# The operand pairs of a seven-product feed-forward: differences on GpSimd, casts behind a copy of the next tile

## The chip, the cores and the metric

One core of one Trainium2 chip. The metric is the device time of one execution in microseconds; lower is better. The kernel before took 2896.02 us, the median of three runs (2888.88 to 2900.18).

## The reference, cut to what matters

One inference step of a two-layer decoder trunk on 576 columns (512 of a prompt, 64 of eight samples), model width 1024, feed-forward width 2816. Each layer has two feed-forward parts; the change touches the first of layer 0 and the second of layer 1.

```python
def swiglu(x, wi, wo):
    gate, up = jnp.split(x @ wi, 2, axis=-1)
    return (jax.nn.silu(gate) * up) @ wo
...
h = h + 0.5 * swiglu(rms_norm(h, w['norm_w'][i, 0]), w['ffn1_wi'][i], w['ffn1_wo'][i])
```

## The kernel before

Everything is kept transposed, 128 features by 576 columns a tile, in two halves of 288 columns. A matrix product in float32 is made of three passes: each operand is split into a rounded part H, a cast on ScalarE, and a remainder L = x - H, a subtraction on DVE or GpSimd, and TensorE sums H*H + H*L + L*H. `split` (L161) does this for moving operands.

A feed-forward part (`ffn`, L395 on) makes 22 tiles j of 128 hidden features: gate and up, silu, their product u (128x576). The first five tiles use plain products (`pair`). From tile 5 on `pair7` (L427) makes gate and up of both column halves as one 2x2 block product with seven products in place of eight, each of 4 x 3 = 12 matmuls of 128x288. In the text the seven are counted in the order in which TensorE runs them. Results are built up in three PSUM banks A, C, B: a bank is copied out by ScalarE (`copy`, L440, its instruction L442) or added to a copy by DVE (`add`, L445, its instruction L448) before the next product adds to it. So the third product waits for the copy of the first, the fifth for the copy of the third, and the seventh for DVE's addition that reads the fifth. After the silu (L152), u is the product of up and silu, one half on DVE (L484), the other on GpSimd (L485).

The weights of a tile are formed by `seven` (L331): four raw blocks come in by DMA on SP's queue, DVE makes four sums and differences of them (L358, L369; the first and third read two SBUF blocks, the others also PSUM), ScalarE casts each of the seven forms (L350), and DVE or GpSimd makes the remainders (L353; forms 0, 3 and 6 on GpSimd). Forms of the next tile are made while a tile runs, as buffers come free.

Two of the four feed-forward parts are "deep" (`deep=True`): their second product, h += 0.5 * (u @ wo), also runs as seven products from the seventh hidden tile on (`wo_part7`, L507). It runs once after tile 14, for tiles 6 to 13, and once after tile 21, for tiles 14 to 21, each time for n = 0, 2, 4, 6. For it two tiles of u, a (even j) and b (odd j), are made into seven moving operands by `pair_forms` (L376): four differences of 128x288 (L382 to L385: c = a1 - a0, then b1 - a1, d = b1 - c0, and a1 = b0 - d), then a split of c, a, b and d. It is called when tile b is complete: the differences on DVE, the casts on ScalarE, the remainders on GpSimd (two of them on DVE for the last pair, `quick`). There are eight pairs in a deep part.

The tile framework orders each engine's queue by its own priorities from the program's order and the dependencies; an engine then works its queue strictly in that order. `after` (L157) adds an order between two instructions of one engine.

Of the kernel before, what the change touches and what calls it, by code (L numbers as in the profile page):

```python
# [9 lines left out]
F32R = mybir.dt.float32r  # L10
# [6 lines left out]
D = 1024  # L17
# [6 lines left out]
FT = FF // 128  # L24
# [69 lines left out]
class Body:  # L94
# [65 lines left out]

    def split(self, src, H, L, eng=None):  # L161
        nc = self.nc
        nc.scalar.copy(H, src)
        self.last_l = (eng or nc.vector).tensor_tensor(L, src, H.bitcast(F32), op=ALU.subtract).ins  # L164
        return H, L
# [209 lines left out]

    def pair_forms(self, a, b, quick):  # L376

        nc = self.nc
        h0, h1 = slice(0, HF), slice(HF, T)
        sub = ALU.subtract  # L380
        c, d = self.s("t1", self.n_t1), self.ph.tile([128, HF], F32, name="ev", tag="ev", bufs=N_EV)
        nc.vector.tensor_tensor(c[:, h0], a[:, h1], a[:, h0], op=sub)  # L382
        nc.vector.tensor_tensor(c[:, h1], b[:, h1], a[:, h1], op=sub)
        nc.vector.tensor_tensor(d, b[:, h1], c[:, h0], op=sub)
        nc.vector.tensor_tensor(a[:, h1], b[:, h0], d, op=sub)  # L385
        out = []
        for i, x in enumerate((c, a, b)):
            out.append(self.split(x, self.s("hv", self.n_hv, F32R), self.s("hv", self.n_hv, F32R), nc.vector if quick and i < 2 else nc.gpsimd))
        D = self.ph.tile([128, 2, HF], F32R, name="hv", tag="hv", bufs=self.n_hv)
        self.split(d, D[:, 0], D[:, 1], nc.gpsimd)  # L390
        C, A, B = out
        return [(x[0][:, sl], x[1][:, sl]) for x, sl in ((C, h0), (C, h1))] + [(D[:, 0], D[:, 1])] + \
            [(x[0][:, sl], x[1][:, sl]) for x, sl in ((A, h1), (A, h0), (B, h0), (B, h1))]

    def ffn(self, wi, wo, done, pre=None, mid=None, fast=None, side=None, deep=False):  # L395

        nc = self.nc
        xs, rs = self.xl[0], self.rs
        hv, hist = {}, {}
# [3 lines left out]
        first7 = ends[1] if deep else FT  # L403
        pairs = {}

# [20 lines left out]

        def pair7(j, X):  # L427
            h0, h1 = slice(0, HF), slice(HF, T)
            n = DT // 2 * 128
# [10 lines left out]
            def copy(ps):  # L440
                t = self.ph.tile([128, HF], F32, name="ev", tag="ev", bufs=N_EV)
                nc.scalar.copy(t, ps)  # L442
                return t
# [25 lines left out]
            else:  # L469
# [4 lines left out]
                prod(A, 2, 2, False)  # L474
                u2 = copy(A)
                prod(B, 3, 5, True)
                add(B, p1, t1[:, h0])
# [9 lines left out]
            if j < first7:  # L487
                hv[j] = self.split(u, self.s("hv", self.n_hv, F32R), self.s("hv", self.n_hv, F32R), nc.gpsimd)
            elif (j - first7) % 2 == 0:
                pairs[j] = u  # L490
            else:
                pairs[j - 1] = self.pair_forms(pairs[j - 1], u, j == FT - 1)

# [13 lines left out]
        def wo_part7(js, last):  # L507

            f = done() if last else None
            X = [pairs[j] for j in js[0::2]]  # L510
            h0, h1 = slice(0, HF), slice(HF, T)
            for n in range(0, DT, 2):
                v = [wo[n + a][:, js[0] * 128:(js[-1] + 1) * 128].rearrange("p (i z c) -> p z i c", z=2, c=128) for a in range(2)]
                W = self.seven({f"{a + 1}{b + 1}": v[a][:, b] for a in range(2) for b in range(2)})
                A, C, B = self.bank("e", HF), self.bank("e", HF), self.pg.tile([128, HF], F32, name="ps_d", tag="d")

                def prod(ps, i, x, first, ks=range(len(X))):
# [5 lines left out]
                def to_h(ps, a, sl):  # L523
                    h = self.h[n + a]
                    return nc.vector.scalar_tensor_tensor(h[:, sl], ps, 0.5, h[:, sl], op0=ALU.mult, op1=ALU.add).ins
                if last and not n:
                    steps = ((C, 1, 0), (A, 0, 4), (B, 3, 5))
# [35 lines left out]
        j = 0  # L563
# [1384 lines left out]
```

## Time and profile before

| what | value |
|---|---|
| median of three runs | 2896.02 us (2888.88 to 2900.18) |
| profiled execution, its own time | 2892.69 us |
| its span, first to last instruction | 2890.9 us |
| mean granted TensorE clock | 0.973 |
| busy: TensorE, DVE, GpSimd, ScalarE | 2724.6, 1848.0, 1395.2, 1329.0 us |
| the first deep part, and the second | about 85 to 438 us, and 2463 to 2823 us of the span |

PE is TensorE's matmuls, PEld its weight loads, DVE VectorE, ACT ScalarE, POOL GpSimd, SP SyncE; L numbers are lines of the kernel. In a timeline row stand the start (us from the span's start), the duration, engine, line, operation, output and inputs, shapes, and in brackets the idle time of the engine just before, with what ended it. A row of a table by stretches gives, for each engine, its busy time and the number of instructions, then the granted TensorE clock as a share of 2.4 GHz, the DMA share and GB/s. The list of waits gives, for each pair of who waited and whom for, the total in us, the number of waits and the longest. DVE's rows of successive instructions overlap slightly, as do the others'.

### The profile page before, as it was taken

How to read it: one execution, taken by the hardware profiler on the slowest of the kernel's cores; microseconds unless marked ns; L12 is line 12 of the kernel's file. 1: busy time of each engine (PE TensorE's matmuls, PEld its weight loads, DVE VectorE, ACT ScalarE, POOL GpSimd, SP SyncE). 2: the span in 40 equal slices, each digit the busy share in tenths (PEclk: the TensorE clock that was granted, in tenths of full speed). 3: DMA queues.
4: the chain of work that ended last, by engine and by line, in shares of the span. 5: the costliest groups of instructions: out<-in, count | busy, mean ns of one | idle time of the engine just before them, and what ended most of it. 6: DMA issues, size and time to landing. Idle time of an engine off the chain costs nothing.

```text
span 2890.9 us, 55999 instructions
## 1 busy us (share of the span) xinstructions
PE 2724.6 (94%) x21760; PEld 2539.6 (88%) x21760; DVE 1848.0 (64%) x3683; ACT 1329.0 (46%) x2648; POOL 1395.2 (48%) x1130
## 2 busy tenths in 40 slices
PE   8999997988999999999999999999999999989997
PEld 7999997887767768999999999999888789989987
DVE  6577788557577756553646546352777776477775
ACT  4344445444333225443445445354556654444454
POOL 5555547544243335544544455454444335564543
PEclk9999998998999999999999999999999999999999
DMA  4223234222112112232333223325334533223222
GB/s 134 82 84 88 85 100 138 70 66 54 53 44 77 39 52 85 83 94 87 94 97 97 94 85 96 92 77 143 90 81 113 161 126 98 88 77 94 79 77 92
DMA packets 201758, 257.80 MB, mean 89 GB/s; under 512 B 46937, under 2 KB 101761, under 8 KB 201492
## 3 DMA queue, kind: packets, MB, share of 16 engines
q1 hardware_dynamic: 173888, 224.74, 25.7%
q10 hardware_dynamic: 27604, 29.48, 3.7%
q8 instruction: 171, 2.80, 0.4%
q14 instruction: 95, 0.78, 0.1%
HBM read 234.31 MB, written 19.85 MB: 88 GB/s over the span
## 4 chain that ended last, share of the span: by engine, by line
PE 75%; DVE 14%; ACT 4%; issue 3%; POOL 2%; DMA 1%; ACTq 0%; DVEq 0%; SPq 0%; POOLq 0%
PE ps_e L205 22%; PE ps_e L438 20%; PE ps_d L649 11%; PE ps_e L521 5%; PE ps_d L438 3%; PE ps_i L649 2%; PE ps_s L649 2%; PE ps_q L649 2%; PE ps_w L649 2%; PE ps_x L649 1%; DVE ps_q L358 1%; PE ps_o L649 1%; PE ps_pt L658 1%; ACT sh L350 1%; DVE S L1448 1%
## 5 line engine op out<-in xcount | busy, mean ns | idle before, releaser
L179 POOL TENSOR_TENSOR wl<-wr,wh 128x512 fp32r<-128x512 f32 (+2 forms) x413 | 521.2, 1272 | 651.7 <-ACT wh L178 617.6
L178 ACT CAST wh<-wr 128x512 fp32r<-128x512 f32 (+2 forms) x413 | 237.6, 582 | 434.7 <-PE ps_e L205 217.1
L205 PE MATMUL ps_e<-hv,wh 128*128 128x288 f32 x1920 | 383.4, 295 | 1.9 <-ACT wh L178 1.3
L649 PE MATMUL ps_d<-x,wh 128*128 128x288 f32 x1664 | 370.0, 309 | 7.8 <-POOL x L164 3.5
L205 PE MATMUL ps_e<-x,wh 128*128 128x288 f32 x1792 | 363.8, 298 | 10.8 <-ACT x L274 7.2
L353 POOL TENSOR_TENSOR wl<-wr,wh 128x512 fp32r<-128x512 f32 x168 | 260.5, 1553 | 150.4 <-ACT wh L350 144.7
L205 PEld LDWEIGHTS ps_e<-hv,wh 128*128 128x128 f32 x1920 | 308.2, 188 | 2.7 <-ACT wh L178 1.5
L205 PEld LDWEIGHTS ps_e<-x,wh 128*128 128x128 f32 x1792 | 290.6, 189 | 12.6 <-ACT x L274 7.2
L649 PEld LDWEIGHTS ps_d<-x,wh 128*128 128x128 f32 x1664 | 274.8, 192 | 28.9 <-issue 9.6
L205 PE MATMUL ps_e<-hv,wl 128*128 128x288 f32 x960 | 283.1, 295 | 1.2 <-POOL wl L179 1.2
L205 PE MATMUL ps_e<-x,wl 128*128 128x288 f32 x896 | 265.0, 297 | 0.0
L649 PE MATMUL ps_d<-x,wl 128*128 128x288 f32 x832 | 250.4, 301 | 0.3 <-POOL wl L179 0.3
L438 PE MATMUL ps_e<-x,wh 128*128 128x288 f32 x1056 | 213.8, 295 | 0.2 <-DVE ev L448 0.2
L438 PE MATMUL ps_e<-TH,wh 128*128 128x288 f32 x544 | 166.8, 307 | 48.7 <-ACT ev L442 39.4
L500 DVE SCALAR_TENSOR_TENSOR h<-ps_e,h 128x288 f32<-128x288 f32 x128 | 58.3, 456 | 195.9 <-PE ps_e L205 195.8
L205 PEld LDWEIGHTS ps_e<-hv,wl 128*128 128x128 f32 x960 | 180.7, 188 | 1.5 <-POOL wl L179 1.4
L485 POOL TENSOR_TENSOR u<-ev,t 128x288 f32<-128x288 f32 x68 | 55.3, 814 | 258.7 <-ACT t L152 241.4
L438 PEld LDWEIGHTS ps_e<-x,wh 128*128 128x128 f32 x1056 | 169.6, 188 | 4.2 <-issue 3.9
L350 ACT CAST sh<-ps_q 128x512 fp32r<-128x512 f32 x168 | 98.3, 585 | 160.6 <-DVE ps_q L358 151.8
L205 PEld LDWEIGHTS ps_e<-x,wl 128*128 128x128 f32 x896 | 169.6, 190 | 0.3
L438 PE MATMUL ps_e<-TH,wl 128*128 128x288 f32 x544 | 165.7, 305 | 0.0
L438 PE MATMUL ps_e<-TL,wh 128*128 128x288 f32 x544 | 165.0, 303 | 0.0
(440 smaller groups left out, 7460.8 us busy)
## 6 DMA issues: line engine op xcount, KB each, us to landing
wr<-in_f1wi SPq DMA_DIRECT2D x108, 256.0 KB
wr<-in_f2wi SPq DMA_DIRECT2D x108, 256.0 KB
sr<-in_f1wi SPq DMA_DIRECT2D x68, 256.0 KB
sr<-in_f2wi SPq DMA_DIRECT2D x68, 256.0 KB
wr<-in_f1wo SPq DMA_DIRECT2D x56, 256.0 KB
wr<-in_f2wo SPq DMA_DIRECT2D x56, 256.0 KB
wr<-in_wrkv SPq DMA_DIRECT2D x48, 256.0 KB
wr<-in_wq SPq DMA_DIRECT2D x48, 256.0 KB
```

What stands on the lines that cost most here:

```text
L178: nc.scalar.copy(H, raw)
L179: nc.gpsimd.tensor_tensor(L, raw, H.bitcast(F32), op=ALU.subtract)
L205: nc.tensor.matmul(ps[0:nw], a, b[:, sl], start=k + m == 0, stop=3 * k + m == n - 1)
L350: c = nc.scalar.copy(H, a).ins
L353: eng.tensor_tensor(L, a, H.bitcast(F32), op=ALU.subtract)
L358: i = nc.vector.tensor_tensor(t, a, b, op=op).ins
L438: nc.tensor.matmul(ps, a, b, start=first and k + m == 0, stop=k == DT // 2 - 1 and m == 2, skip_group_check=True)
L485: nc.gpsimd.tensor_tensor(u[:, h1], c22, t1[:, h1], op=ALU.mult)
L500: nc.vector.scalar_tensor_tensor(h[:, sl], ps, 0.5, h[:, sl], op0=ALU.mult, op1=ALU.add)
L521: nc.tensor.matmul(ps, a, b, start=first and k + m == 0, stop=k == len(X) - 1 and m == 2, skip_group_check=True)
L649: self.nc.tensor.matmul(out, lhsT, rhs, **kw)
L658: self.nc.tensor.transpose(out, in_, ident)
```

## The change

`pair_forms` is no longer called when tile b is complete. The pair is put on a list, `waiting`, and `form_pair` takes it from there inside the next tile's `pair7`, after the copy of that tile's third product is written down. It hands that copy on as `behind`: then the four differences go to GpSimd, all remainders go to GpSimd, and each of the four casts is ordered after the copy in ScalarE's queue. A pair with no further tile (the last one) is formed at the start of `wo_part7`, without `behind`: differences and two remainders on DVE as before. In `wo_part7` the order of products in which the last pair's operands come late, so far used in the last call alone, is now used for n = 0 of both calls.

```diff
-    def split(self, src, H, L, eng=None):
+    def split(self, src, H, L, eng=None, behind=None):
         nc = self.nc
-        nc.scalar.copy(H, src)
+        c = nc.scalar.copy(H, src).ins
+        if behind is not None:
+            self.after(c, behind)
...
-    def pair_forms(self, a, b, quick):
+    def pair_forms(self, a, b, behind=None):
...
-        nc.vector.tensor_tensor(c[:, h0], a[:, h1], a[:, h0], op=sub)
-        nc.vector.tensor_tensor(c[:, h1], b[:, h1], a[:, h1], op=sub)
-        nc.vector.tensor_tensor(d, b[:, h1], c[:, h0], op=sub)
-        nc.vector.tensor_tensor(a[:, h1], b[:, h0], d, op=sub)
+        eng = nc.gpsimd if behind is not None else nc.vector
+        eng.tensor_tensor(c[:, h0], a[:, h1], a[:, h0], op=sub)
+        eng.tensor_tensor(c[:, h1], b[:, h1], a[:, h1], op=sub)
+        eng.tensor_tensor(d, b[:, h1], c[:, h0], op=sub)
+        eng.tensor_tensor(a[:, h1], b[:, h0], d, op=sub)
         out = []
         for i, x in enumerate((c, a, b)):
-            out.append(self.split(x, ..., nc.vector if quick and i < 2 else nc.gpsimd))
+            out.append(self.split(x, ..., nc.vector if behind is None and i < 2 else nc.gpsimd, behind))
...
-        self.split(d, D[:, 0], D[:, 1], nc.gpsimd)
+        self.split(d, D[:, 0], D[:, 1], nc.gpsimd, behind)
...
-        pairs = {}
+        pairs, waiting = {}, []
+
+        def form_pair(behind=None):
+            if waiting:
+                i, u = waiting.pop()
+                pairs[i] = self.pair_forms(pairs[i], u, behind)
...
             def copy(ps):
                 t = self.ph.tile([128, HF], F32, name="ev", tag="ev", bufs=N_EV)
-                nc.scalar.copy(t, ps)
+                self.last_c = nc.scalar.copy(t, ps).ins
                 return t
...
                 u2 = copy(A)
+                form_pair(self.last_c)
                 prod(B, 3, 5, True)
...
-                pairs[j - 1] = self.pair_forms(pairs[j - 1], u, j == FT - 1)
+                waiting.append((j - 1, u))
...
-            X = [pairs[j] for j in js[0::2]]
+            X = []
...
                 A, C, B = self.bank("e", HF), self.bank("e", HF), self.pg.tile([128, HF], F32, name="ps_d", tag="d")
+                if not n:
+                    form_pair()
+                    X += [pairs[j] for j in js[0::2]]
...
-                if last and not n:
+                if not n:
                     steps = ((C, 1, 0), (A, 0, 4), (B, 3, 5))
```

How the queues move is shown at tile 8, which follows the pair of tiles 6 and 7; the other tiles behind a pair read alike. (Names: u_1129 is a, u_1691 is b, t1 is c, the small ev next to it is d, hv the seven operands' tiles; wh/wl and sh/sl are the H and L of weight forms, wr/sr raw weights, ps_q and ps_d sums of them in PSUM. Lines of the changed kernel stand 2 to 12 higher.)

**ScalarE, tile 8, before**, from the last cast of the tile's own weights to its third copy (ev_1902):

```order
L350 CAST wh_1853<-wr_1817 128x512
L163 CAST hv_1798<-t1_1792 128x576
L350 CAST wh_1967<-wr_1959 128x512
L442 COPY ev_1874<-ps_e_1859 128x288
L163 CAST hv_1802<-u_1129 128x576
L350 CAST sh_1973<-ps_q_1971 128x512
L163 CAST hv_1806<-u_1691 128x576
L442 COPY ev_1888<-ps_e_1860 128x288
L163 CAST hv_1810<-ev_1793 128x288
L350 CAST sh_1983<-sr_1965 128x512
L442 COPY ev_1902<-ps_e_1859 128x288
```

and with the change, from the second copy to the tile's silu:

```order
L450 COPY ev_1867<-ps_e_1839 128x288
L352 CAST wh_1979<-ps_q_1977 128x512
L450 COPY ev_1881<-ps_e_1838 128x288
L163 CAST hv_1889<-t1_1883 128x576
L163 CAST hv_1893<-u_1129 128x576
L352 CAST sh_1995<-ps_q_1993 128x512
L163 CAST hv_1897<-u_1691 128x576
L352 CAST wh_1989<-ps_d_1987 128x512
L163 CAST hv_1901<-ev_1884 128x288
L152 ACTIVATE t1_1836<-t1_1836 128x576
```

The four casts stood among the three copies; now they stand behind the third, and ahead of the casts of two weight forms of tile 9 and of the silu.

**GpSimd, tile 8, before**, from b's second half to that of tile 8:

```order
L485 TENSOR_TENSOR u_1691<-ev_1762,t1_1690 128x288
L353 TENSOR_TENSOR wl_1854<-wr_1817,wh_1853 128x512
L164 TENSOR_TENSOR hv_1799<-t1_1792,hv_1798 128x576
L353 TENSOR_TENSOR wl_1968<-wr_1959,wh_1967 128x512
L164 TENSOR_TENSOR hv_1803<-u_1129,hv_1802 128x576
L164 TENSOR_TENSOR hv_1807<-u_1691,hv_1806 128x576
L164 TENSOR_TENSOR hv_1810<-ev_1793,hv_1810 128x288
L353 TENSOR_TENSOR sl_1984<-sr_1965,sh_1983 128x512
L485 TENSOR_TENSOR u_1858<-ev_1929,t1_1857 128x288
```

and with the change:

```order
L385 TENSOR_TENSOR t1_1883<-u_1129 128x288
L494 TENSOR_TENSOR u_1691<-ev_1762,t1_1690 128x288
L386 TENSOR_TENSOR t1_1883<-u_1691,u_1129 128x288
L355 TENSOR_TENSOR wl_1833<-wr_1796,wh_1832 128x512
L355 TENSOR_TENSOR wl_1968<-wr_1959,wh_1967 128x512
L355 TENSOR_TENSOR sl_1984<-sr_1965,sh_1983 128x512
L387 TENSOR_TENSOR ev_1884<-u_1691,t1_1883 128x288
L388 TENSOR_TENSOR u_1129<-u_1691,ev_1884 128x288
L166 TENSOR_TENSOR hv_1890<-t1_1883,hv_1889 128x576
L166 TENSOR_TENSOR hv_1894<-u_1129,hv_1893 128x576
L166 TENSOR_TENSOR hv_1898<-u_1691,hv_1897 128x576
L166 TENSOR_TENSOR hv_1901<-ev_1884,hv_1901 128x288
```

The four differences are new here, three weight remainders stand between the second and the third of them, and the four remainders of the pair follow in one row, all ahead of tile 8's own second half.

**DVE, tile 8, before**, from the fourth weight difference of tile 9 to the product u:

```order
L358 TENSOR_TENSOR ps_q_1993<-sr_1965,ps_q_1977 128x512
L448 TENSOR_TENSOR ev_1929<-ps_e_1859,ev_1888 128x288
L353 TENSOR_TENSOR sl_1996<-ps_q_1993,sh_1995 128x512
L353 TENSOR_TENSOR wl_1990<-ps_d_1987,wh_1989 128x512
L448 TENSOR_TENSOR t1_1857<-ps_e_1860,ev_1902 128x288
L484 TENSOR_TENSOR u_1858<-ps_e_1859,t1_1857 128x288
```

and with the change:

```order
L360 TENSOR_TENSOR ps_q_1993<-sr_1965,ps_q_1977 128x512
L456 TENSOR_TENSOR t1_1836<-ps_d_1840,ev_1853 128x288
L355 TENSOR_TENSOR sl_1996<-ps_q_1993,sh_1995 128x512
L456 TENSOR_TENSOR ev_1929<-ps_e_1838,ev_1867 128x288
L355 TENSOR_TENSOR wl_1990<-ps_d_1987,wh_1989 128x512
L456 TENSOR_TENSOR t1_1836<-ps_e_1839,ev_1881 128x288
L493 TENSOR_TENSOR u_1837<-ps_e_1838,t1_1836 128x288
```

The addition into ev_1929, which the seventh product waits for, stood ahead of the weight remainder sl_1996; now it stands behind it, and sl_1996 needs the cast sh_1995, which stands behind the pair's cast hv_1893 on ScalarE.

## Rows read from the trace of the kernel before

**Rows 1.** The profile's page, part 1: busy us (share of the span) xinstructions.

```profile
PE 2724.6 (94%) x21760; PEld 2539.6 (88%) x21760; DVE 1848.0 (64%) x3683; ACT 1329.0 (46%) x2648; POOL 1395.2 (48%) x1130
```

**Rows 2.** List of waits: who <- whom: us in total, times, longest.

```profile
ACT hv L163 <- DVE u L385: 46.0, 14, 3.3
...
PE ps_e L438 <- ACT ev L442: 39.4, 17, 2.8
```

**Rows 3.** Stretches between fourth products, 14 without a pair; one, and sum.

```profile
176.65:187.77 11.12, 11.12 (x87) 11.12 (x86) 8.86 (x14) 4.86 (x9) 6.55 (x6) 1.00 0.31 108
...
sum 155.79, PE 155.79 PEld 155.79 DVE 116.83 ACT 68.07 POOL 82.26; mean PE 11.13 PEld 11.13 DVE 8.34 ACT 4.86 POOL 5.88
```

**Rows 4.** The same, 12 behind a pair; the first two, and sum.

```profile
162.54:176.65 14.11, 11.44 (x87) 11.21 (x85) 11.12 (x16) 8.16 (x17) 9.77 (x8) 1.00 0.24 66
187.77:203.47 15.70, 12.92 (x86) 12.69 (x85) 11.72 (x16) 8.38 (x17) 10.52 (x9) 0.89 0.23 66
...
sum 185.01, PE 152.12 PEld 149.38 DVE 138.62 ACT 100.25 POOL 124.47; mean PE 12.68 PEld 12.45 DVE 11.55 ACT 8.35 POOL 10.37
```

**Rows 5.** The same, tile 14 with the second product; sum of two.

```profile
sum 118.91, PE 113.43 PEld 112.97 DVE 87.87 ACT 49.52 POOL 57.57; mean PE 56.72 PEld 56.49 DVE 43.93 ACT 24.76 POOL 28.79
```

**Rows 6.** Timeline of TensorE in tile 10, at its fifth product.

```profile
192.28 0.40 PE L438 MATMUL ps_e<-TH,wh 128*128 128x288 f32 x1 [2.78 <-ACT ev L442]
```

**Rows 7.** Timeline of ScalarE in tile 10.

```profile
189.05 0.67 ACT L163 CAST hv<-u 128x576 fp32r<-128x576 f32 x1 [3.29 <-DVE u L385]
189.63 0.58 ACT L350 CAST sh<-ps_q 128x512 fp32r<-128x512 f32 x1
...
191.82 0.41 ACT L442 COPY ev<-ps_e 128x288 f32<-128x288 f32 x1
```

**Rows 8.** DVE: timeline, tile 10; all L385 (ns min/median/max); timeline, tile 11.

```profile
184.52 1.19 DVE L384 TENSOR_TENSOR ev<-u,t 128x288 f32<-128x288 f32 x1
...
L385 DVE TENSOR_TENSOR u<-u,ev x16: 450/1542/1546, 162.1 to 2769.1; 128x288 f32<-128x288 f32 x16
...
199.34 0.69 DVE L358 TENSOR_TENSOR ps_q<-sr,wr 128x512 f32<-128x512 f32 x1
```

**Rows 9.** Timeline in tile 9: ScalarE's third copy, TensorE's seventh product.

```profile
177.24 0.40 ACT L442 COPY ev<-ps_e 128x288 f32<-128x288 f32 x1
...
181.41 0.43 PE L438 MATMUL ps_e<-x,wh 128*128 128x288 f32 x2
```

**Rows 10.** Timeline of GpSimd from tile 10 to tile 11.

```profile
182.94 0.81 POOL L485 TENSOR_TENSOR u<-ev,t 128x288 f32<-128x288 f32 x1 [4.50 <-ACT t L152]
...
185.36 1.64 POOL L164 TENSOR_TENSOR hv<-t,hv 128x576 fp32r<-128x576 f32 x1
186.97 1.74 POOL L353 TENSOR_TENSOR wl<-wr,wh 128x512 fp32r<-128x512 f32 x1
189.80 2.77 POOL L164 TENSOR_TENSOR hv<-u,hv 128x576 fp32r<-128x576 f32 x2 [1.09 <-ACT hv L163]
192.53 1.25 POOL L164 TENSOR_TENSOR hv<-ev,hv 128x288 fp32r<-128x288 f32 x1
193.74 1.28 POOL L353 TENSOR_TENSOR sl<-sr,sh 128x512 fp32r<-128x512 f32 x1
...
199.50 1.68 POOL L353 TENSOR_TENSOR wl<-wr,wh 128x512 fp32r<-128x512 f32 x1
```

**Rows 11.** Timeline in tile 9: ScalarE's cast, DVE's remainder, DVE's addition.

```profile
178.78 0.59 ACT L350 CAST sh<-ps_q 128x512 fp32r<-128x512 f32 x1 [1.14 <-DVE ps_q L358]
...
179.40 0.69 DVE L353 TENSOR_TENSOR sl<-ps_q,sh 128x512 fp32r<-128x512 f32 x1
180.01 0.46 DVE L448 TENSOR_TENSOR ev<-ps_e,ev 128x288 f32<-128x288 f32 x1
```

**Rows 12.** Stretch around the stop of TensorE in tile 5.

```profile
93.00:97.00 4.00, 3.19 (x24) 3.07 (x24) 3.60 (x7) 2.47 (x5) 2.83 (x3) 1.00 0.40 123
```

**Rows 13.** Timeline of TensorE at the start of the last second product.

```profile
393.84 0.40 PE L521 MATMUL ps_e<-hv,wh 128*128 128x288 f32 x1 [1.64 <-DVE hv L164]
```

More of the change, by code (lines that the diff above doesn't have):

```diff
@@ L381, in pair_forms @@
         c, d = self.s("t1", self.n_t1), self.ph.tile([128, HF], F32, name="ev", tag="ev", bufs=N_EV)
-        nc.vector.tensor_tensor(c[:, h0], a[:, h1], a[:, h0], op=sub)
-        nc.vector.tensor_tensor(c[:, h1], b[:, h1], a[:, h1], op=sub)
-        nc.vector.tensor_tensor(d, b[:, h1], c[:, h0], op=sub)
-        nc.vector.tensor_tensor(a[:, h1], b[:, h0], d, op=sub)
+        eng = nc.gpsimd if behind is not None else nc.vector
[3 more added lines that the diff above has]
+        eng.tensor_tensor(a[:, h1], b[:, h0], d, op=sub)
         out = []
         for i, x in enumerate((c, a, b)):
-            out.append(self.split(x, self.s("hv", self.n_hv, F32R), self.s("hv", self.n_hv, F32R), nc.vector if quick and i < 2 else nc.gpsimd))
+            out.append(self.split(x, self.s("hv", self.n_hv, F32R), self.s("hv", self.n_hv, F32R), nc.vector if behind is None and i < 2 else nc.gpsimd, behind))
         D = self.ph.tile([128, 2, HF], F32R, name="hv", tag="hv", bufs=self.n_hv)
-        self.split(d, D[:, 0], D[:, 1], nc.gpsimd)
+        self.split(d, D[:, 0], D[:, 1], nc.gpsimd, behind)
         C, A, B = out
```

## The prediction, made before the changed kernel ran

> **What bounds the kernel now.** I read the page first: TensorE is busy 94% of the span [rows 1], so only idle time of TensorE, or time at its lower clock, can be won. The list of waits then says who makes TensorE wait in the seven-product tiles (L438): it waits for ScalarE's copies at L442, 39.4 us in 17 waits, while ScalarE itself waits 46.0 us in 14 waits for L385, the last difference of `pair_forms` [rows 2]. Fourteen is the number of pairs formed ahead of another gate/up tile (two feed-forward parts of eight pairs, the last pair of each being followed by the second product instead).
>
> The table by stretches gives the price. Each stretch runs from the fourth product of one tile to that of the next. Without a pair between them a tile takes 11.12 us, on average 155.79 / 14 = 11.13 [rows 3]. The tile after an odd one (I call it the carrier: 8, 10, 12, 14, 16, 18, 20) takes 14.11 us in two cases and about 15.7 in ten; these twelve sum to 185.01 us [rows 4]. The other two carriers are followed by the second product, so I take their stretches with it: 118.91 us for what is ten tiles' worth of matmuls (84 each) [rows 5]. So the excess is 185.01 - 12 x 11.13 = 51.5, and 118.91 - 10 x 11.13 = 7.6: **59.1 us in all**, 4.2 per pair.
>
> Where it comes from is seen in one carrier, tile 10. TensorE stops 2.78 us before its fifth product, until a copy at L442 [rows 6]. That copy is the third of the tile, and ScalarE reaches it only at 191.82, because the cast of the second operand at 189.05 stood idle 3.29 us for DVE's L385 and everything behind it in the queue stood too [rows 7]. L385 is late because DVE's differences of two SBUF operands, 0.45 us at best, take 1.19 and 1.54 there [rows 8]. In ten of twelve cases TensorE's granted clock averages 0.89 over the stretch (1.00 in the other two and in all without a pair): it fell to 1.2 GHz after the stop, and cost 15.7 - 14.1 = 1.6 us more [rows 4].
>
> **The change, part by part.** *Casts behind the third copy.* The order of ScalarE's queue shows all three copies ahead of the four casts. In tile 9, which carries no pair, the third copy starts at 177.24, 0.59 us after the fourth product, and TensorE is busy for the whole 11.12 us [rows 3, 9]; with nothing of the pair ahead of the copy the same holds in the carriers. The 2.7 us stop before the fifth product goes, and with it the 1.6 us of clock: -59.1 us at most.
>
> *Differences on GpSimd.* Four instructions of 128x288 per pair leave DVE and join GpSimd. Nothing in the trace does this very step there; the nearest row is L485 with 0.81 us [rows 10], and the contended end is the 1.25 us of a 128x288 low at L164 with a DVE step of two SBUF operands beside it [rows 10]. I take 0.81, because three of the four have no DVE difference of two SBUF operands beside them any more, and add the price of the one that does. GpSimd has the room in the sum: per two tiles 2 x 0.81 + 4 x 0.81 + 6 x 1.28 for the weights + 1.64 + 2.77 + 1.25 for the four lows [rows 10] = 18.2 us, in 22.3 us.
>
> *What is late next.* The order in GpSimd's queue puts three weight lows between the second and the third difference, the second operand's cast on ScalarE waits for the fourth, and behind that cast now stand the sixth weight form's cast, DVE's low of it, and, behind that on DVE, the addition into `ev` (L448) that frees the bank of the seventh product. I walk it through tile 10 with its own times. Its L485 ends at 182.94 + 0.81 = 183.75 [rows 10]. Then the second difference (0.81, plus 0.40 since DVE's sum of two raw weights falls beside it: a weight low of 1.28 took 1.68 so), two weight lows at 1.28, one at 1.74 with the next such DVE step beside it, and two differences at 0.81, all from [rows 10]: 1.21 + 2.56 + 1.74 + 1.62 = 7.13, less some 0.2 because successive rows overlap: 190.7. From there: 0.58 until ScalarE is at the next cast (189.63 - 189.05 [rows 7]), 0.62 until DVE starts the low, 0.61 until it starts the addition (178.78, 179.40, 180.01), 0.46 for it [rows 11]: 193.0. The seventh product would start 4.76 us after the fourth (181.41 - 176.65 [rows 3, 9]), at 187.77 + 4.76 = 192.5. So a new stop of **0.5 us** before the seventh product, 14 times: +7 us. Bounds: without a contended step 6.3 us instead of 7.1, so no stop (0); with each of the six at its contended length (3 x 1.25 + 3 x 1.74 = 9.0) 192.7 and a stop of 2.5 us. I stay near the lower end, as DVE has only two such steps in that time.
>
> A stop of 0.5 us should not cost clock: the 0.81 us stop of tile 5 stands in a stretch of granted clock 1.00: 3.19 us busy of 4.00 [rows 12]. The activation of the carrier comes some 0.7 us later than in an undisturbed tile, about where it stands now in a stopped one, and the tiles behind those show no stop.
>
> In [rows 8, 10] a GpSimd step beside a DVE step of two SBUF operands is longer by 0.40 to 0.46 us, and the DVE step may be too (L384, L385). The Trainium skill ("SBUF — State Buffer", SBUF: two separate sides) calls this an exclusive lock on a port pair that the two engines share, held for the whole instruction. By that rule, and the trace agrees that they take turns, each of the two meetings would cost GpSimd DVE's full 0.69 us, the stop would be 1.0 us and the time 2848, still inside the forecast's own range; for the price I keep the rows.
>
> *Second product.* Its first output pair now always runs three operand pairs ahead of the last one. For the first of its two calls this is new: the last low of pair 13 lands about 190.7 + 5.7 = 196.4 in tile 10's terms, 13.4 us after the tile's start; the product begins at 11.6 and asks for that operand 27 matmuls (3.6 us) later, at 15.2. Cost 0; bounds: 0, and the 1.64 us that the other call of this code stops now [rows 13], twice, 3.3 us. The last pair keeps DVE and its place in the queues: 0. No transfer is added; four issues on SP change places between weight loads that are a tile ahead: 0.
>
> **Sum.** 2892.7 (the profiled execution, of which 2890.9 is span) - 59.1 + 7.0 = 2840.6. The median of three runs, 2896.0, lies 3.3 above the profiled one, within their spread; I put the forecast at **2842**.
>
> **The rivals.**
> *A, nothing left over (0.17).* GpSimd's steps meet DVE less than I assume, the stop before the seventh product vanishes: 2892.7 - 59.1 = 2834. For it: the walk misses by 0.5 us only. Against: both meetings that it leaves out stand in the rows of a neighbouring tile [rows 8, 10].
> *B, a longer stop that brings the clock down (0.13).* If the fourth difference ends 1 us later than I think, the stop is 1.5 us; if that brings the clock down as the stops do now, it is 3.1 us per pair: 2892.7 - 59.1 + 43 = 2877.
> *C, GpSimd becomes the bound (0.03 slower).* With every step contended GpSimd needs 2 x 0.81 + 4 x 1.25 + 6 x 1.74 + 5.7 = 22.8 us per two tiles, more than the 22.3 TensorE needs; that sum is the point from which it decides. Then the stop is 2.5 + 1.6 in each carrier, and in the tile behind it DVE's first sum waits as it does now in carriers (by the length of a GpSimd low, some 1.2 us), which holds ScalarE's first copy back as much: 5.3 to 5.4 us per pair, 2892.7 - 59.1 + 75 = 2909. The Trainium skill leans this way ("GPSIMD Engine Reference", Engine selection): a two-input elementwise step belongs on VectorE, GpSimd being about half as fast. The rows agree on the ratio (0.81 against 0.45), but at those lengths GpSimd fits.
> *D, given back entirely (0.05).* The carriers stop 2.5 us at the new place and lose the clock as now, or the copies turn out to wait for something else: 2891.
>
> **How the numbers follow.** Forecast 0.62, A 0.17, B 0.13, D 0.05, C 0.03. A measurement of this kernel tells about 0.5% from no change, which is 14.5 us: the first three are faster (0.92), D is the same, C slower. The range starts 5 us below A, for the spread of the runs, and goes over the forecast's own upper end (a stop of 1.1 us, 2849, and the spread) into the lower part of B: 2829 to 2866.
>
> **What would show it.** Right: no stop before the fifth product, stretches of carriers at 11.1 to 12.2 us with granted clock 1.00, TensorE waiting at L438 for DVE's addition instead of ScalarE's copy, GpSimd without long idle stretches in carriers. Wrong: stretches still above 14 us; granted clock 0.89 again; TensorE waiting for a GpSimd weight low; a stop in the tiles without a pair, or above 2 us at the start of the second product.

## The result, and the profile after

The changed kernel takes **2853.95 us** (median of four runs, 2846.31 to 2856.06) against 2895.67 us for the kernel before (2888.88 to 2900.18) in the same job: a ratio of **0.9853**, 95% interval 0.9826 to 0.988. It is faster by 42 us, where the forecast of 2842 stood for 54; the time lies inside the stated range, 12 us above the forecast. The profiled execution took 2853.55 us, of which 2851.7 are span.

The profile's page, part 1, of the changed kernel [rows 1 before], and from its part 5 the group that waits most in the deep tiles:

```profile
PE 2712.0 (95%) x21760; PEld 2524.7 (89%) x21760; DVE 1762.2 (62%) x3627; ACT 1330.4 (47%) x2648; POOL 1429.0 (50%) x1186
...
L446 PE MATMUL ps_e<-x,wh 128*128 128x288 f32 x1056 | 215.1, 297 | 9.4 <-DVE ev L456 9.4
```

56 instructions (14 pairs x 4) have gone from DVE to GpSimd. TensorE no longer waits for ScalarE's copy in the carriers [rows 2]; it waits 9.4 us for DVE's addition at L456, which is L448 of the kernel before.

The table by stretches, fourth product to fourth product, of the twelve carriers that are followed by a tile [rows 4 before]: two of them (322.20 is the longest) and the sum; then one of the two stretches of tile 14 with the second product, and the sum of both [rows 5 before].

```profile
184.47:196.53 12.06, 11.43 (x87) 11.19 (x85) 6.71 (x12) 7.64 (x15) 11.98 (x11) 1.00 0.27 88
...
322.20:334.53 12.33, 11.39 (x87) 11.16 (x86) 7.36 (x13) 7.65 (x15) 12.25 (x11) 1.00 0.29 88
...
sum 145.04, PE 136.94 PEld 134.13 DVE 81.02 ACT 91.75 POOL 144.10; mean PE 11.41 PEld 11.18 DVE 6.75 ACT 7.65 POOL 12.01
...
230.90:287.88 56.98, 56.35 (x422) 55.77 (x421) 40.59 (x72) 23.81 (x43) 29.89 (x24) 1.00 0.32 97
...
sum 114.16, PE 112.83 PEld 111.63 DVE 81.00 ACT 47.60 POOL 59.87; mean PE 56.42 PEld 55.82 DVE 40.50 ACT 23.80 POOL 29.94
```

The carriers fell from 14.1 and 15.7 us to 12.0 to 12.3, and the granted clock is 1.00 in all of them. The excess, by the prediction's own sum, is now 145.04 - 12 x 11.13 = 11.5 and 114.16 - 10 x 11.13 = 2.9, together **14.3 us instead of 59.1**. GpSimd, busy 124.47 of 185.01 us in carriers before [rows 4], is busy 144.10 of 145.04.

What the 0.94 us of a carrier are can be read in tile 10 of the changed kernel (its fourth product starts at 184.47). The timeline of TensorE, GpSimd, ScalarE and DVE, one after the other:

```profile
190.03 0.40 PE L446 MATMUL ps_e<-x,wh 128*128 128x288 f32 x1 [0.63 <-DVE ev L456]
...
179.53 0.81 POOL L494 TENSOR_TENSOR u<-ev,t 128x288 f32<-128x288 f32 x1 [3.90 <-ACT t L152]
180.41 1.28 POOL L386 TENSOR_TENSOR t<-u 128x288 f32<-128x288 f32 x1
181.65 3.07 POOL L355 TENSOR_TENSOR wl<-wr,wh 128x512 fp32r<-128x512 f32 x2
184.69 1.29 POOL L355 TENSOR_TENSOR sl<-sr,sh 128x512 fp32r<-128x512 f32 x1
185.94 0.81 POOL L387 TENSOR_TENSOR ev<-u,t 128x288 f32<-128x288 f32 x1
186.82 0.80 POOL L388 TENSOR_TENSOR u<-u,ev 128x288 f32<-128x288 f32 x1
...
185.06 0.41 ACT L450 COPY ev<-ps_e 128x288 f32<-128x288 f32 x1
185.35 0.69 ACT L163 CAST hv<-t 128x576 fp32r<-128x576 f32 x1
187.66 0.68 ACT L163 CAST hv<-u 128x576 fp32r<-128x576 f32 x1 [1.62 <-POOL u L388]
188.24 0.58 ACT L352 CAST sh<-ps_q 128x512 fp32r<-128x512 f32 x1
...
188.92 0.69 DVE L355 TENSOR_TENSOR sl<-ps_q,sh 128x512 fp32r<-128x512 f32 x1 [2.07 <-ACT sh L352]
189.53 0.45 DVE L456 TENSOR_TENSOR ev<-ps_e,ev 128x288 f32<-128x288 f32 x1
```

The third copy (185.06) starts 0.59 us after the fourth product, as in an undisturbed tile [rows 9]. Behind it the cast of `a` stands idle 1.62 us for the fourth difference (L388), then come the next tile's weight form, DVE's remainder of it, DVE's addition at 189.53, and 0.05 us behind its end the seventh product. This is the chain of the prediction, link by link. The stop is there 14 times, 0.61 to 0.94 us.

### The profile page after: what moved, and what is told of

It reads as the page before. It is cut to its first block, busy times and chain, and to the rows that moved or that the text cites. A ratio compares the mean times of both kernels' runs of the same rounds, so it can differ in the third digit from the quotient of the medians.

```text
span 2851.7 us, 56073 instructions
## 1 busy us (share of the span) xinstructions
PE 2712.0 (95%) x21760; PEld 2524.7 (89%) x21760; DVE 1762.2 (62%) x3627; ACT 1330.4 (47%) x2648; POOL 1429.0 (50%) x1186
## 4 chain that ended last, share of the span: by engine, by line
PE 76%; DVE 13%; issue 4%; ACT 3%; POOL 2%; DMA 1%; SPq 0%; ACTq 0%; DVEq 0%; POOLq 0%
PE ps_e L207 22%; PE ps_e L446 20%; PE ps_d L661 11%; PE ps_e L533 5%; PE ps_d L446 3%; PE ps_i L661 2%; PE ps_s L661 2%; PE ps_q L661 2%; PE ps_w L661 2%; PE ps_x L661 1%; PE ps_o L661 1%; PE ps_pt L670 1%; DVE S L1460 1%; PE ps_d L533 1%; DVE ps_q L360 1%
## 5 line engine op out<-in xcount | busy, mean ns | idle before, releaser
L661 PE MATMUL ps_d<-x,wh 128*128 128x288 f32 x1664 | 371.5, 310 | 7.1 <-POOL x L166 3.0
L661 PEld LDWEIGHTS ps_d<-x,wh 128*128 128x128 f32 x1664 | 276.9, 193 | 28.1 <-issue 9.7
L207 PEld LDWEIGHTS ps_e<-x,wh 128*128 128x128 f32 x1792 | 290.8, 190 | 11.5 <-ACT x L276 6.9
L661 PE MATMUL ps_d<-x,wl 128*128 128x288 f32 x832 | 251.6, 303 | 0.3 <-POOL wl L181 0.3
L355 DVE TENSOR_TENSOR sl<-ps_q,sh 128x512 fp32r<-128x512 f32 x168 | 115.5, 688 | 85.5 <-ACT sh L352 85.1
L661 PEld LDWEIGHTS ps_d<-x,wl 128*128 128x128 f32 x832 | 160.5, 193 | 2.2 <-issue 0.5
```

Source lines behind the costliest of these rows:

```text
L207: nc.tensor.matmul(ps[0:nw], a, b[:, sl], start=k + m == 0, stop=3 * k + m == n - 1)
L355: eng.tensor_tensor(L, a, H.bitcast(F32), op=ALU.subtract)
L661: self.nc.tensor.matmul(out, lhsT, rhs, **kw)
```

## The experiments

All ratios are to the kernel before, run in the same job. **Theory:** the time was lost because ScalarE's copies stood behind casts that waited for a late difference, and what is left is the chain above. **Rival 1:** the gain comes from DVE being relieved of the differences. **Rival 2:** what is left is DVE and GpSimd getting in each other's way, whatever the order. **Rival 3:** the 5 or 6 us between the deep parts' gain and the profiled executions' gain belong to the change.

| run | edit | median us | ratio, 95% interval |
|---|---|---|---|
| | the changed kernel | 2853.95 | 0.9853 (0.9826 to 0.988) |
| e8 | the same, again | 2848.45 | 0.9842 (0.9826 to 0.9858) |
| e6 | kernel before, differences on GpSimd only | 2887.12 | 0.9978 (0.9966 to 0.999) |
| e3 | only formed in the next tile | 2858.46 | 0.9865 (0.984 to 0.9889) |
| e1 | that, and casts ordered; differences on DVE | 2860.91 | 0.9885 (0.9865 to 0.9906) |
| e2 | that, and GpSimd; casts not ordered | 2891.72 | 0.9987 (0.997 to 1.0004) |
| e9 | changed kernel, third difference twice | 2861.81 | 0.9891 (0.9873 to 0.9909) |
| e7 | changed kernel, second product's edit undone | 2850.73 | 0.9847 (0.9826 to 0.9867) |
| e4 | changed kernel, two GpSimd remainders behind the pair | 2838.94 | 0.9798 (0.9771 to 0.9824) |
| e5 | changed kernel, DVE's addition ahead of the remainder | 2838.41 | 0.9807 (0.9792 to 0.9822) |
| e10 | e4, e5 and e7 together | 2832.64 | 0.9796 (0.9781 to 0.9811) |

### Which part of the change gains: e6, e3, e1, e2

e6, in `pair_forms` of the kernel before (the last pair stays on DVE):

```diff
+        eng = nc.vector if quick else nc.gpsimd
-        nc.vector.tensor_tensor(c[:, h0], a[:, h1], a[:, h0], op=sub)
+        eng.tensor_tensor(c[:, h0], a[:, h1], a[:, h0], op=sub)
...
```

> The kernel before with the four differences moved to GpSimd and nothing else: pair_forms stands where it stood, so the casts stay ahead of ScalarE's copies. My theory: the engine alone gives nothing, because the casts of a, b and d still stand ahead of the third copy and wait for a fourth difference that ends no earlier on GpSimd: stops of 2.5 to 4 us before the fifth product or the copies' other consumers, 2885 to 2920. The rival that relieving DVE is what gains: the stop shrinks by a microsecond or more and the clock with it, 2860 or less.

Measured 2887.12, at the lower edge of what the theory gave. TensorE's and ScalarE's timeline in tile 10 of e6:

```profile
189.07 0.40 PE L439 MATMUL ps_e<-TH,wh 128*128 128x288 f32 x1 [2.47 <-ACT ev L443]
...
188.04 0.67 ACT L163 CAST hv<-u 128x576 fp32r<-128x576 f32 x1 [1.59 <-POOL u L386]
188.62 0.39 ACT L443 COPY ev<-ps_e 128x288 f32<-128x288 f32 x1
```

The stop for a copy is there in all 14 carriers, 2.42 to 2.48 us, but at another place than before: it is now the tile's first copy that comes late, and TensorE stops before the third product, 2.0 us ahead of the fourth (191.07). The copy stands behind the cast, and whether DVE or GpSimd makes the cast wait hardly matters. Rival 1 falls in its plain form.

e3 undoes the ordering and the engine:

```diff
-        c = nc.scalar.copy(H, src).ins
-        if behind is not None:
-            self.after(c, behind)
+        nc.scalar.copy(H, src)
...
-        eng = nc.gpsimd if behind is not None else nc.vector
+        eng = nc.vector
```

> Both statements undone: differences on DVE, casts not ordered; only the place in the program where pair_forms is written (in the next tile, behind the second copy) is left of the change. My theory: the copies are ahead of the casts of a, b and d here too, so nearly the whole gain is in this one edit: 2840 to 2856, no stop before the fifth product. If GpSimd or the ordering is needed, the stops of 2.7 us remain: about 2890.

Measured 2858.46, 2 us above the theory's range and far from the rival's 2890: **most of the gain, 36 of 42 to 44 us, comes from where `pair_forms` is written.** In the next tile, behind the third copy, its casts of `a`, `b` and `d` get a place in ScalarE's queue behind the copies without being told to. (The second product's edit is still in e3; e7 shows that it saves nothing.)

e1 undoes the engine alone:

```diff
-        eng = nc.gpsimd if behind is not None else nc.vector
+        eng = nc.vector
```

> The changed kernel with one part undone: the four differences run on DVE again, the casts stay ordered behind the third copy. My theory: the gain comes from ScalarE's copies, which no longer stand behind casts that wait for a late difference; it needs no GpSimd. In DVE's order the fourth difference stands ahead of the weight form's second remainder, so it is done before the cast that needs it, and the addition that frees the seventh product's bank no longer hangs on GpSimd. No stop before the fifth product, none or under 0.3 us before the seventh, carriers at 11.1 to 11.5 us, 14 x 0.93 = 13 us below the changed kernel: about 2841. The rival that the gain comes from relieving DVE: DVE's differences of 1.2 to 1.5 us come back, the additions behind them are late, the stop of 2.7 us shows up before the sixth or seventh product, and the time is about 2890.

Measured 2860.91: 20 us above what I expected. The stop before the fifth product is gone and the one before the seventh is down to 0.19 to 0.24 us, both as forecast, but others took their place: TensorE now stops for ScalarE's first copy, before the third product. The table by stretches of e3 (behind the fourth product of a carrier, then of the odd tile after it), and from its timeline the stop and DVE's rows ahead of it:

```profile
161.80:173.41 11.61, 11.41 (x87) 11.19 (x86) 9.61 (x15) 6.86 (x14) 9.06 (x8) 1.00 0.23 78
173.41:185.35 11.94, 11.41 (x86) 11.17 (x85) 9.08 (x15) 6.27 (x12) 7.15 (x6) 1.00 0.32 103
...
183.66 0.40 PE L444 MATMUL ps_e<-TH,wh 128*128 128x288 f32 x1 [0.53 <-ACT ev L448]
...
180.52 0.46 DVE L384 TENSOR_TENSOR t<-u 128x288 f32<-128x288 f32 x1 [1.70 <-POOL u L492]
180.89 0.45 DVE L491 TENSOR_TENSOR u<-ps_e,t 128x288 f32<-128x288 f32 x1
181.26 1.43 DVE L358 TENSOR_TENSOR ps_q<-sr,wr 128x512 f32<-128x512 f32 x1
```

DVE's second difference stands 1.70 us idle for GpSimd's product of the other half; behind it in DVE's queue wait two steps, the second of them (L358) stretched from 0.69 to 1.43 us, and behind that ScalarE's first cast and first copy, 0.53 us too late for TensorE. The tiles lose 0.5 to 0.8 us so (in e1, with 11.97 and 12.27, 0.8 to 1.1). So relieving DVE does gain, in combination: it takes another head of a queue away. The Trainium skill ("GPSIMD Engine Reference", Engine selection) would have such elementwise steps on VectorE. Here, with the casts behind the copies, GpSimd is the better place by 7 to 12 us (e1 against the two medians of the changed kernel, from two jobs), since it is the waiting in DVE's queue that costs, not the length of the step.

e2 undoes the ordering alone:

```diff
-        c = nc.scalar.copy(H, src).ins
-        if behind is not None:
-            self.after(c, behind)
+        nc.scalar.copy(H, src)
```

> The changed kernel without the ordering of the four casts: differences on GpSimd, formed in the next tile. ScalarE's order then has only the cast of c ahead of the first copy; the casts of a, b and d stand behind the third copy anyway, because pair_forms is now written in the next tile. My theory: what counts is the cast of a, which waits for the last difference, and it is behind the copies here too; so the same time as the changed kernel, 2854 within 10, with a stop of up to 0.5 us before the third product where the cast of c waits for GpSimd's second difference (up to 7 us in all). The rival that the stated order of all four casts is what removes the stop: 2.7 us stops are back in the carriers and the time is near 2890.

Measured 2891.72: no gain at all. My theory as I had put it fell here, and the rival's place is wrong too: no stop stands before the fifth product. The only stops for a copy are the small ones that I had allowed for, 0.16 to 0.24 us before the third product of 13 carriers (184.85 in tile 10); with them the stretch from the odd tile's fourth product to the carrier's takes 11.62 us, 0.5 more than before. Stretches of two carriers of e2, TensorE's stop in tile 10 (fourth product at 186.56), and the timelines of GpSimd and ScalarE:

```profile
161.50:174.94 13.44, 11.42 (x87) 11.19 (x86) 7.48 (x12) 7.07 (x14) 11.86 (x11) 1.00 0.25 80
186.56:201.56 15.00, 12.95 (x86) 12.71 (x85) 6.63 (x12) 7.17 (x14) 12.05 (x11) 0.89 0.23 72
...
193.53 0.40 PE L444 MATMUL ps_e<-x,wh 128*128 128x288 f32 x1 [2.05 <-DVE ev L454]
...
184.52 1.42 POOL L164 TENSOR_TENSOR hv<-t,hv 128x576 fp32r<-128x576 f32 x1
185.91 1.74 POOL L353 TENSOR_TENSOR wl<-wr,wh 128x512 fp32r<-128x512 f32 x1
...
189.75 0.81 POOL L386 TENSOR_TENSOR u<-u,ev 128x288 f32<-128x288 f32 x1
...
190.59 1.25 ACT L163 CAST hv<-u 128x576 fp32r<-128x576 f32 x2 [3.03 <-POOL u L386]
191.74 0.58 ACT L350 CAST sh<-ps_q 128x512 fp32r<-128x512 f32 x1
```

It is the chain of the changed kernel, 1.4 us longer. The early cast of `c` lets its remainder (184.52) into GpSimd's queue ahead of the last two differences, so that the fourth ends 190.56 - 186.56 = 4.00 us after the fourth product instead of 187.62 - 184.47 = 3.15; and ScalarE runs the cast of `b` together with that of `a`, so that the weight form starts 191.74 - 190.56 = 1.18 us after that difference instead of 0.62. 0.85 + 0.56 = 1.41, and the stop went from 0.63 to 2.05. In 7 of the 12 stretches the clock falls as well (15.00 against 13.44). **The stated place is not what frees the copies; it keeps the remainder of `c` and the cast of `b` out of the chain.** The two shares are read from these rows; no run moved one of the two alone.

### What is left: e9, e4, e5

e9, in `pair_forms`:

```diff
-        eng.tensor_tensor(d, b[:, h1], c[:, h0], op=sub)
+        for _ in range(1 if behind is None else 2):
+            eng.tensor_tensor(d, b[:, h1], c[:, h0], op=sub)
```

> The changed kernel with the pair's third difference computed twice on GpSimd, which puts the fourth later by one instruction, about 0.85 us, and changes nothing else in any queue. By the chain of my theory the stop before the seventh product grows from 0.65 by the same 0.85 to 1.5 us, carriers from 12.05 to 12.9: 14 x 0.85 = 12 us, 2850 + 12 = 2862, if the granted clock stays at 1.00 after a stop of 1.5 us. If a stop of that length is followed by a fall of the clock, as stops of 2.0 us were in 9 of 14 places of the run with the casts unordered, each such place costs 1.5 us more: up to 2883. The rival that the stop does not hang on the fourth difference: no growth, 2850.

Measured 2861.81. The stops are 1.49 to 1.59 us and one of 1.80, carriers 12.88 to 13.01 and one of 13.2, the clock 1.00. Two stretches of e9, the second with its longest stop, and GpSimd's fourth difference in the first:

```profile
185.12:198.05 12.93, 11.41 (x86) 11.18 (x85) 6.68 (x12) 7.64 (x15) 12.77 (x12) 1.00 0.26 79
326.45:339.67 13.22, 11.42 (x87) 11.19 (x86) 7.32 (x13) 7.64 (x15) 13.06 (x12) 1.00 0.24 79
...
188.35 0.81 POOL L389 TENSOR_TENSOR u<-u,ev 128x288 f32<-128x288 f32 x1
```

In tile 10 (the first of the two) the fourth difference ends 189.16 - 185.12 = 4.04 us after the fourth product, 0.89 later than in the changed kernel, and the stretch is 0.87 longer: the chain passes it on in full.

e4, in `form` of `seven`, with `self.last_d` set to the pair's last difference:

```diff
+            if i in (0, 3) and self.last_d is not None:
+                self.after(l, self.last_d)
...
```

> The changed kernel with two of GpSimd's weight remainders of the next tile (forms 0 and 3) ordered behind the pair's last difference, so that the fourth difference ends 1 to 3 us earlier. My theory of what is left: the stop of 0.65 us before the seventh product, 0.93 us per pair with what goes with it, is the chain fourth difference on GpSimd, cast of a, sixth weight form's cast, DVE's remainder, DVE's addition. Then the stop vanishes and the time falls by 14 x 0.93 = 13 us to about 2841, unless the two delayed remainders hold up the next tile's first products, which would show as a stop there. The rival that the addition is late because DVE meets GpSimd's steps at all, in whatever order they stand: the stop stays at 0.6 us and the time at 2854.

e5, in the same place, with `self.last_a` the addition of the tile before:

```diff
+            if i == 5 and self.last_a is not None:
+                self.after(l, self.last_a)
...
```

> The changed kernel with one thing moved on DVE alone: the remainder of the weight form that waits for the cast behind the cast of a stands behind the addition that frees the seventh product's bank, instead of ahead of it. GpSimd, ScalarE and SyncE keep their order. My theory, by which the stop of 0.65 us before the seventh product is the tail of the chain fourth difference, cast of a, weight form's cast, DVE's remainder, addition: the addition now depends on the fifth product alone, the stop vanishes with GpSimd's order unchanged, carriers at 11.1 to 11.2 us, about 2841 like the run with GpSimd's remainders behind the differences (2839). The rival that what helped there was GpSimd's order as such (its lows no longer beside DVE's steps): the stop stays and the time is 2854.

Both came out as the theory had it, 2838.94 and 2838.41. Stretches of a carrier and of an odd tile, first of e4:

```profile
162.93:174.05 11.12, 11.12 (x87) 11.12 (x86) 7.50 (x12) 7.54 (x15) 11.12 (x10) 1.00 0.25 89
174.05:185.16 11.11, 11.11 (x87) 11.11 (x85) 6.81 (x12) 5.70 (x11) 7.90 (x8) 1.00 0.30 104
```

and of e5:

```profile
161.17:172.48 11.31, 11.31 (x86) 11.18 (x85) 7.14 (x12) 7.44 (x15) 11.23 (x11) 1.00 0.26 82
172.48:183.63 11.15, 11.15 (x87) 11.15 (x85) 6.67 (x12) 5.70 (x11) 7.88 (x7) 1.00 0.33 104
```

e5 speaks against rival 2: GpSimd and ScalarE keep their order, GpSimd is as busy beside DVE as before (11.23 of 11.31 us), and the stop is gone because the addition no longer stands behind a step that waits. Its carriers still take 11.3 to 11.4 us, 0.2 to 0.3 above a tile without a pair; in tile 10 that is lost before the next tile's third product (193.26), whose weight load waits 0.17 us for ScalarE's copy. e4 cuts the same chain two links earlier; its fourth difference ends 185.86 - 185.16 = 0.70 us after the fourth product. DVE's order there also came out with the addition ahead of the remainder, so e4 alone would not tell which of the two did it; e9 and e5 do.

### The second product, the spread, the sum: e7, e8, e10

e7, in `wo_part7`:

```diff
-                if not n:
+                if last and not n:
                     steps = ((C, 1, 0), (A, 0, 4), (B, 3, 5))
```

> The changed kernel with its second-product edit undone: the first output pair of the first of the two calls runs its operand pairs in one row of products as before, the other call keeps the form that runs the last operand pair last. My prediction put this edit at 0 (bounds 0 to 3.3 us) with the last low of pair 13 landing 13.4 us after its tile's start, 1.8 us after the product begins. By that, undoing it makes the first product wait: a stop of 1 to 2 us at the start of the second product, twice, and 2 to 6 us more in all, 2856 to 2860, if the clock stays up. If pair 13's operands are there anyway, nothing: 2854.

Measured 2850.73, the same as the changed kernel. The two stretches of tile 14 with the second product are shorter by 0.98 us together (114.16 above):

```profile
sum 113.18, PE 111.89 PEld 111.42 DVE 80.53 ACT 48.21 POOL 61.22; mean PE 55.95 PEld 55.71 DVE 40.27 ACT 24.10 POOL 30.61
```

The edit cost half a microsecond per call and saved nothing. I had let the first products wait for the pair's last remainder, but that is of `d`, which the products use later; the first one uses a half of `a`. In e7 the remainders of `a` and `b` end at 235.32 + 2.81 = 238.13 on GpSimd, and the first product's matmuls on that pair run at 239.29.

e8 is the changed kernel again, with no edit:

> The changed kernel unaltered, once more, for its spread and a second trace. If the missing 6 us between the gain within the two deep parts (44.5 us) and the gain of the profiled executions (39.1 us) is chance of one execution, the stop of 3.9 us that the first trace shows among the recurrent layer's matmuls is not there again or stands elsewhere, and the stretch between the two deep parts is again somewhere in the 2086 to 2097 us that the six traces so far show. If it belongs to the change, it stands at the same matmul again. Median 2854 within 4.

Measured 2848.45, profiled execution 2845.24, 8.3 us less than the first profile of the same kernel, with the same carriers (12.01 to 12.35). Most of the difference, 7.2 us, lies between the deep parts. Stretch from the last fourth product of the first part to the first of the second, in the changed kernel's first profile, then in e8's:

```profile
357.75:2452.99 2095.24, 1999.03 (x16530) 1821.31 (x16529) 1301.98 (x2853) 962.65 (x1962) 967.83 (x805) 0.98 0.30 89
```

```profile
358.18:2446.26 2088.08, 1998.16 (x16530) 1821.32 (x16529) 1303.90 (x2853) 962.76 (x1962) 969.52 (x805) 0.98 0.30 89
```

The kernel before took 2088.77 there, the other nine 2086 to 2097, and the code is the same in all. In the first profile of the changed kernel a matmul of the recurrent layer (L661, 635.78) stops 3.89 us for DVE's L970; e8 has only a stop of 1.13 us a few matmuls on, for the same L970, and e5 has the 3.89 again. Rival 3 falls: this stretch comes out one way or another, execution by execution.

e10 puts the edits of e4, e5 and e7 together:

> The changed kernel with the three single edits that took time off it put together: GpSimd's weight remainders of forms 0 and 3 behind the last difference, DVE's remainder of form 5 behind the addition, and the second product's first output pair as before in its first call. The first two remove the same stop, so they do not add: the carriers are at 11.1 already with the first. The third took 0.4 us off each of two calls. 2837, no more than 2 us below the runs with one of the first two (2838 and 2839), which the spread hides.

Measured **2832.64** (2829.39 to 2837.76), ratio 0.9796: 21 us below the first median of the changed kernel, 6 below e4 and e5, more than the 2 expected. A carrier of e10, and the sum of its two stretches of tile 14 with the second product:

```profile
172.89:184.00 11.11, 11.11 (x86) 11.11 (x85) 6.68 (x12) 5.70 (x11) 7.88 (x8) 1.00 0.34 106
```

```profile
sum 111.39, PE 111.39 PEld 111.39 DVE 80.58 ACT 48.02 POOL 61.59; mean PE 55.70 PEld 55.70 DVE 40.29 ACT 24.01 POOL 30.80
```

All excess of pairs is gone: 111.39 against 10 x 11.13 = 111.3. About 2 of the 6 us are the second product's (these two stretches sum to 113.5 us in e4 and in e5), and against e5 another 3 are the carriers' (133.4 us for the twelve, 136.4 in e5); the rest is of the size of the spread, and the run does not tell it from that.

## Why the prediction was right, and where it was short

*The stop before the fifth product goes, and the clock's loss with it: right.* No carrier stops there, and the granted clock is 1.00 in all fourteen. That the third copy starts 0.59 us after the fourth product came out to the hundredth. But I gave the stated place the credit; e3 shows that writing `pair_forms` in the next tile does it alone.

*Differences on GpSimd at 0.81 us, one of them contended at 1.21: right.* In the profile three of the four take 0.81 on average, and the second takes 1.25 to 1.28 in 13 of 14 pairs. GpSimd takes them in the time it had idle, and rival C did not come.

*The new stop, its place and its chain: right; its size is the term that was mis-sized, 0.5 us per pair where 0.96 were lost (11.48 / 12).* Four pieces make the difference. The walk over GpSimd, from the end of the carrier's first GpSimd step to the end of the fourth difference, took 187.62 - 180.34 = 7.28 us instead of 6.95. It met DVE just where I had put it, in the second difference (1.28, not 1.21) and in one of the three weight remainders (3.07 + 1.29 = 4.36 for the three, not 4.30), and the six steps sum to 7.25 instead of 7.13; the larger error is the 0.2 us that I had taken off for overlapping rows, since small gaps make up for the overlaps (7.28 for rows that sum to 7.25). GpSimd's start was 0.1 earlier, relative to the fourth product. From there to the seventh product it took 190.03 - 187.62 = 2.41 instead of 2.27. And my price of a stop was its lateness alone: the seventh product came 5.56 - 4.76 = 0.80 us late, the row shows 0.63 us idle, and the stretch lost 0.94, because the row counts idle time only from the end of the last matmuls, and the first two matmuls after it took 0.54 us instead of 0.43.

*Second product at 0 (bounds 0 to 3.3): short by 1.0 us in all* (e7), for the wrong reason.

*The sum.* 59.1 - 14.3 = 44.8 us gained in the deep parts, where 52.1 were forecast: 7.3 of the 12 us missing. The other 5 are mostly the stretch between the deep parts, 6.5 us longer in the profiled execution than in that of before, by chance; the second job's median, 2848.45, is without most of it.

*The exclusive lock.* By the rule of the Trainium skill ("SBUF — State Buffer", SBUF: two separate sides) I had put the stop at 1.0 us and the time at 2848. The size is close to what was lost, but its reason is not in the rows: the contended difference took 1.25 to 1.28 us, 0.44 to 0.47 more than alone, not DVE's whole 0.69 more. That the two take turns, the trace agrees, with rows of e3 and e4 in the last section.

*The rivals.* A, nothing left over, is what e4 and e5 make of the change (2839 against the 2834 stated). B was tried by e9: its stop of 1.5 us is there to the tenth, the fall of the clock is not, and it costs 1.8 us in tile 10 (12.93 - 11.13), not 3.1. D, all given back, is what e2 does, one statement away from the change: a stop of 2.05 us at the new place, with the clock falling at most of them. I had given it 0.05 and no mechanism that would produce it; the queue of GpSimd with the remainder of `c` in it was one.

## What to carry to other kernels

On an engine that takes its queue in order, price what stands *behind* a waiting step, and follow the chain to the last engine: here the late step was one, its victims were a copy, then an addition, and moving the victim ahead in its own queue (e5) was worth as much as making the late step earlier (e4). When work moves to another engine, look also at what can now enter that engine's queue ahead of it: the place of two casts on ScalarE, one of which let a remainder into GpSimd's queue, decided the whole gain. A stop costs more than its idle time in the row, by some 0.3 us here, and before it is priced with the clock, look how long the stops are that were followed by a fall, and how many of that length were not.

## What had not been expected of the hardware

The seventh product's stops of 0.61 to 1.80 us, 42 in three profiles (the changed kernel twice, e9), left the granted clock at 1.00, 2.4 GHz, every time. Longer ones were followed by a fall to 1.2 GHz in some cases and not in others: those of 2.01 to 2.50 us in e2 in 9 of 14 (in 7 of the 12 stretches), those of 2.42 to 2.48 us in e6 in 9 of 14, those of 2.66 to 2.78 us in the kernel before in 11 of 14 (in 10 of the 12 of [rows 4]). The length of the stop alone does not decide it: e2's longest, 2.50 us, left the clock at 1.00. A fall costs 15.00 - 13.44 = 1.56 us here.

When DVE and GpSimd meet in steps of two SBUF operands, the one that begins second pays in these rows, first two of e4, then two of e3:

```profile
183.63 0.69 DVE L375 TENSOR_TENSOR ps_d<-wr,sr 128x512 f32<-128x512 f32 x1
183.64 1.34 POOL L391 TENSOR_TENSOR ev<-u,t 128x288 f32<-128x288 f32 x1
...
185.46 1.74 POOL L353 TENSOR_TENSOR sl<-sr,sh 128x512 fp32r<-128x512 f32 x1
185.97 1.54 DVE L385 TENSOR_TENSOR ev<-u,t 128x288 f32<-128x288 f32 x1
```

In e4 DVE began first and took the 0.69 us that it takes alone, and GpSimd's difference took 1.34 instead of 0.81. In e3 DVE's third difference, 0.45 us alone, began while a GpSimd remainder ran and took 1.54; that remainder had itself begun while a step of DVE's ran (L369, 184.55 to 186.06), and took 1.74 instead of 1.29. DVE lost more here, beside a step of 1.29 us, than GpSimd beside steps of 0.69. The smallest steps suffer most: between the deep parts of the changed kernel, beside GpSimd's remainders (629.75, four of them, which end at 635.32), DVE's steps on 72x14 and 72x26 elements took 1.26 and 1.33 us (the latter ends at 635.36), and the one that fell between two of the remainders took 0.17.

```profile
630.30 1.01 DVE L1054 COPY iv<-iv 72x256 f32<-72x256 f32 x1 [5.79 <-DMA iv<-dE]
...
632.53 0.17 DVE L1059 TENSOR_TENSOR iv<-iv 72x14 f32<-72x14 f32 x1
632.74 1.26 DVE L1060 TENSOR_TENSOR iv<-iv 72x14 f32<-72x14 f32 x1
634.03 1.33 DVE L1059 TENSOR_TENSOR iv<-iv 72x26 f32<-72x26 f32 x1
635.28 0.44 DVE L970 TENSOR_SCALAR p<-ps_w 128x288 f32<-128x288 f32 x1
...
629.75 5.57 POOL L166 TENSOR_TENSOR x<-n,x 128x576 fp32r<-128x576 f32 x4 [10.30 <-ACT x L163]
```

The step behind them, L970, is the one that the stop of 3.89 us waited for. That DVE had stood 5.79 us for a transfer first (630.30), and that the moment it lands decides whether the two meet, is my reading of why this stretch differs between executions of one kernel; no run tested it.
